# First retention output projection: first column pair by seven block products, interleaved with the next head's q and k, and the shared residual memory in two halves

## Chip, cores and metric

The kernel runs on one core of a Trainium2 chip. The metric is the device time of one execution in microseconds (us). The kernel before takes 1374.24 us (median of 3 runs, 1373.81 to 1374.61).

## What is computed

A decoder trunk of two layers over 256 tokens and a width of 2048: first gated linear attention (GLA), then retention. Both project the normalised input to q, k, v and a gate, mix over the tokens by head, multiply by the SiLU of the gate and project back with an output matrix; a residual add follows. The retention layer has 8 heads with 256 key and 512 value columns each.

```python
h = x
h = h + gla_mixer(rms_norm(h, gla_norm), ...)
h = h + retention_mixer(rms_norm(h, ret_norm), positions, ...)
return rms_norm(h, final_norm)

def retention_mixer(h, positions, w_in, gn_g, gn_b, w_out):
    q, k, v, gate = jnp.split(h @ w_in, ...)      # 8 heads
    q, k = apply_rotary(q, cos, sin), apply_rotary(k, cos, sin)
    ...                                           # decayed scores @ v, group norm
    return (o * jax.nn.silu(gate)) @ w_out        # (256 x 4096) @ (4096 x 2048)
```

## The kernel before

**Work of one weight block.** The weights come in blocks ("subs") of 256 contraction rows by 512 columns, 512 KB each. SP loads a block into a `raw` buffer (L260). ACT copies it, rounded, to `hi` (L298), DVE writes the rest, raw minus hi, to `lo` (L299), and PE multiplies three times: activations-hi by hi, hi by lo, and lo by hi (`mm3`, `three`: L340 to L342 and L411 to L413). There are four `hi` and four `lo` buffers, and `next_weights` keeps three blocks ahead (LOOK). The list of all loads and blocks is fixed by `_plan`, which also gives each load its buffer: eight `raw` buffers, and two more (`lc` and `qk`, the SPARE table) in stages where the tiles that own them are idle.

**Direct and seven-product pairs.** A 512-column output for all 256 tokens takes 12 matmuls of 512 columns a block (two token halves, two 128-row tiles, three terms) and eight blocks, so two column groups take 192. A *pair* (`pair` in `_plan`, `out_pair`, `values_and_gates`) treats two column groups at once. The second half of the contraction is done directly (tokens v4 to v7 for one group, g4 to g7 for the other, 12 matmuls each). The first half is a 2x2 block product that is done with seven block products instead of eight (P1, P2, P3, P5, P6, P7, P8, each of two blocks and 12 matmuls). So a pair takes 96 + 84 = 180 matmuls, but 22 blocks: products read a block for 6 matmuls only. Four products use sums of activation blocks (`make_sums`, four tiles), and their weight sums are made by adding one raw block to another: by DVE (L293, before P6) and by accumulating DMAs that POOL issues (L310), six a pair. Results of products that enter two outputs are added to the residual straight from PSUM (`join`, L990 and L992), 512 columns each.

**The stages around the change.** Retention head h consists of eight q/k blocks (`step_w`: eight matmuls of 512 columns and eight of 256 a block) and one pair for v and gate. In heads 1 to 3 and 5 to 7 the two are interleaved (order MIXED), in heads 0 and 4 all q/k blocks come first (WHOLE). The attention work of a head (`ret_tasks`: rotary, scores, norm, transposes into `ogt`) is spread over the next stage. The output projection is done in two halves of the contraction: after heads 0 to 3 ("ra", this is where the change lies) and after heads 4 to 7 ("rb"). In ra, column groups 0 and 1 are direct (`out_half` with CUT: six blocks of group 0, six of group 1, then the rest, since head 3 is still being finished), and groups 2 and 3 are a pair (`out_pair(2)`). The sums of `ogt` (`rsum`) are made in the direct part.

**One memory, two tenants.** The `rs` memory (16 KB a partition, one buffer) holds in turn the residual (256 tokens by 2048) and the four sums of the layer's input `xhl` (`sums`), both 2 MB. Before ra the sums are in it, with a copy in HBM (`keep_sums`, L469). `get_resid` (L480, POOL) brings the residual, after ra `put_resid` (L485, ACT's queue) writes it to HBM, and `reload_sums` (L476, POOL) brings the sums back for head 4, whose first use of them is P3, after eight q/k blocks.

**Order.** Each engine works through its instructions in the order in which they stand. A scheduler at build time moves some of them; `keep` pins what must not move. DMAs that POOL issues stand in POOL's order, so one that must wait holds up those behind it.

Of the kernel before, what the change touches and what calls it, by code (L numbers as in the profile page):

```python
# [57 lines left out]
SPARE = {"lc": ("ao", "rqk", "rv", "rg", "ro"), "qk": ("ao", "ro")}  # L58


def _spare(load):
    return [NRAW + n for n, kinds in enumerate(SPARE.values()) if load[0][0] in kinds]


def _plan():
# [96 lines left out]
def ret_order(h):  # L162
    return MIXED if h % 4 else WHOLE
# [15 lines left out]
def kernel(  # L179
# [252 lines left out]
    def sums_in_rs(name):  # L432
        s = rs_p.tile([P, 4, QK, 2, P], F32R, tag="rs", name=name)
        cur["s_whole"] = s
        return lambda n: s[:, 2 * n : 2 * n + 2]
# [30 lines left out]

    def keep_sums(name):
        kept = dram_p.tile([P, 4 * QK * 2 * P], F32R, tag=name, name=f"{name}_kept")
        keep(nc.gpsimd.dma_start(kept, cur["s_whole"].rearrange("p i k a t -> p (i k a t)")))  # L469
        cur["kept"] = kept  # L470

    def reload_sums(name):
        room = sums_in_rs(name)
        cur["s"] = [room(i // 2)[:, i % 2] for i in range(4)]
        s = cur["s_whole"]
        nc.gpsimd.dma_start(s.rearrange("p i k a t -> p (i k a t)"), cur["kept"])  # L476

    def get_resid(name):
        r = rs_p.tile([P, 2, D], F32, tag="rs", name=name)
        nc.gpsimd.dma_start(r, cur["resid_at"])  # L480
        cur["resid"] = r

    def put_resid(name):
        at = dram_p.tile([P, 2, D], F32, tag=name, name=name)
        nc.scalar.dma_start(at, cur["resid"])  # L485
        cur["resid_at"] = at
# [19 lines left out]
    cur["resid"] = rs_p.tile([P, 2, D], F32, tag="rs", name="resid")  # L506
# [90 lines left out]
    def square_sum(t, c):  # L597
        junk = sg_p.tile([P, GW], F32, tag="sg", name="sqj")
        return nc.scalar.activation(
            junk, cur["resid"][:, t, c * GW : (c + 1) * GW], AF.Square, accum_out=ssum[:, t, c : c + 1]  # L600
# [43 lines left out]
    def gate_low_rank():  # L644
        for t in range(2):
            keep(nc.sync.dma_start(cur["resid"][:, t, :], x_n[:, t, :]))
# [311 lines left out]
    def out_cols(c, ps, t, first, final):  # L958
        dst = cur["resid"][:, t, c * GW : (c + 1) * GW]
# [8 lines left out]
    def out_transposes(c):  # L968
        return transpose_out(
            lambda t, j: cur["resid"][:, t, c * GW + j * P : c * GW + (j + 1) * P],  # L970
# [6 lines left out]
    def out_pair(c, first, name, final=False):  # L977
# [9 lines left out]
        def join(col, t, src, op=ALU.add):  # L987
            dst = cur["resid"][:, t, col * GW : (col + 1) * GW]
# [7 lines left out]
        def whole(col, t, now=False):  # L996
# [5 lines left out]
            if final:  # L1002
                keep(a)
                dst = cur["resid"][:, t, col * GW : (col + 1) * GW]
# [13 lines left out]
        direct(lhs, (C, V1), 4)  # L1018
        join(g, 0, A)
# [48 lines left out]
    def out_last(name):  # L1068
# [10 lines left out]
        for t in range(2):  # L1079
            dst = cur["resid"][:, t, 3 * GW : 4 * GW]  # L1080
# [41 lines left out]
    def out_tail():  # L1122
# [4 lines left out]
        for t in range(2):  # L1127
# [20 lines left out]
            for n in range(2):  # L1148
                dst = cur["resid"][:, t, base + n * half : base + (n + 1) * half]
# [9 lines left out]
            for piece, src, which in (  # L1159
# [6 lines left out]
                src = cur["resid"][:, t, piece] if src is None else src  # L1166
# [137 lines left out]
    def ret_head(h):  # L1304
        lhs = xhl
        mixed = h % 4 != 0
        at = (2, 3, 0, 1) if h < 4 else (0, 1, 2, 3)
        q_ps = [acc(1, f"rqk{h}_ps{c}", (P, 2, SEQ), [at[c + 2]])[0] for c in range(2)]
        q_ps += [lev_p.tile([P, 2, SEQ], F32, tag="lev", name=f"rqk{h}_ps{c}") for c in (2, 3)]
        if not mixed:  # L1310
            q_ps = q_ps[2:] + q_ps[:2]
        r, r2 = r2_[:, 0, :], r2_[:, 1, :]
# [17 lines left out]

        def tile_of(key, pool_, shape, dtype, name):
# [14 lines left out]
        def turn(tok):  # L1346
            n = toks.index(tok)
            if n == drain:
# [113 lines left out]
    slots = deque((0, 1, 2, 3))  # L1462
# [115 lines left out]
```

## Time and profile before

| What | Value |
|---|---|
| median of the runs | 1374.24 us |
| the profiled execution | 1373.05 us, of which its span (first to last instruction) is 1371.3 us |
| PE busy | 1362.1 us (99%), 6564 matmuls |
| DVE / ACT / POOL busy | 1099.5 (80%) / 845.8 (62%) / 136.8 us (10%) |
| granted TensorE clock | 0.998 |
| moved by DMA | 315.03 MB, mean 230 GB/s |
| head 3 / ra direct / ra pair / q,k of head 4 / pair of head 4 | first matmul at 855.7 / 918.9 / 967.7 / 1008.7 / 1031.0 us |

The profile names groups of instructions by line, engine, operation and tile (buffer numbers left out); "<-" in a bracket names who ended the idle time before. PE's matmuls overlap, so the duration of one is more than its share of the time; how far apart they start is its share. An instruction that issues a DMA is short, and the time to landing is listed apart.

### The profile page before, as it was taken

To read this page: it belongs to the slowest core of one execution; us is meant where nothing else is said; L and a number is where in the kernel's file an instruction comes from. 1 tells how busy PE (TensorE), PEld (TensorE's weight loads), DVE (VectorE), ACT (ScalarE), POOL (GpSimd) and SP (SyncE) were. 2 spreads that over 40 slices of the span, in tenths; PEclk is the share of its full clock that TensorE was granted. 3 is DMA by queue.
4 is the path that set the end of the run, shared out by engine and by line. 5 is a ranking of instruction groups with operands and counts; after the bars stand their busy time and mean duration, and the time that the engine had idled before them with its cause. 6 is when DMAs were issued, how large, how long until landed. Compare 5 with 4: busy or idle time off the path is not lost.

```text
span 1371.3 us, 18373 instructions
## 1 busy us (share of the span) xinstructions
PE 1362.1 (99%) x6564; PEld 1144.2 (83%) x6564; DVE 1099.5 (80%) x1523; ACT 845.8 (62%) x1115; POOL 136.8 (10%) x194
## 2 busy tenths in 40 slices
PE   9999999999999999999999999999999999999997
PEld 8888888888888888888888888888888888888886
DVE  7686795987878896869888888897867897889796
ACT  6576656656567757656666566655546666666565
POOL 1003020110021021001011010100101101010010
PEclk9999999999999999999999999999999999999999
DMA  9755565789658667868897878796798797869773
GB/s 367 254 173 167 171 206 184 162 245 320 196 153 265 203 205 176 322 169 236 271 324 198 259 201 252 207 321 210 176 360 225 239 262 198 254 201 323 234 179 121
DMA packets 84507, 315.03 MB, mean 230 GB/s; under 512 B 9776, under 2 KB 10800, under 8 KB 83136
## 3 DMA queue, kind: packets, MB, share of 16 engines
q1 hardware_dynamic: 67200, 241.63, 50.3%
q0 software_dynamic: 15920, 64.89, 23.8%
q10 hardware_dynamic: 1296, 7.35, 1.5%
q8 instruction: 51, 0.84, 0.2%
q14 instruction: 40, 0.33, 0.1%
HBM read 303.35 MB, written 10.49 MB: 229 GB/s over the span
## 4 chain that ended last, share of the span: by engine, by line
PE 99%; DVE 0%; ACT 0%; issue 0%; DVEq 0%; POOL 0%; POOLq 0%
PE rqk_ps L383 8%; PE re_ps L411 8%; PE re_ps L412 8%; PE re_ps L413 8%; PE rqk_ps L384 4%; PE gqk_ps L383 4%; PE gg_ps L341 3%; PE gv_ps L342 3%; PE gv_ps L340 3%; PE gv_ps L341 3%; PE gg_ps L340 3%; PE gg_ps L342 3%; PE ge_ps L413 2%; PE ge_ps L411 2%; PE ge_ps L412 2%; PE gae_ps L413 2%
## 5 line engine op out<-in xcount | busy, mean ns | idle before, releaser
L299 DVE TENSOR_TENSOR lo<-raw,hi 128x1024 fp32r<-128x1024 f32 (+1 forms) x567 | 686.6, 1221 | 215.8 <-ACT hi L298 206.7
L298 ACT ACTIVATE hi<-raw 128x1024 fp32r<-128x1024 f32 (+1 forms) x567 | 595.7, 1057 | 396.5 <-DMA raw<-in_w_all 53.4
L383 PE MATMUL rqk_ps<-xhl,hi 128*128 128x512 f32 x480 | 162.8, 397 | 0.0
L412 PE MATMUL re_ps<-lo,xhl 128*128 128x512 f32 x352 | 137.3, 390 | 0.0
L413 PE MATMUL re_ps<-hi,xhl 128*128 128x512 f32 x352 | 137.1, 389 | 0.0
L310 POOL DMA_DIRECT2D raw<-in_w_all x90 | 78.0, 868 | 555.4 <-DVE lo L299 354.3
L411 PE MATMUL re_ps<-hi,xhl 128*128 128x512 f32 x352 | 132.4, 391 | 0.0
L384 PE MATMUL rqk_ps<-xhl,lo 128*128 128x256 f32 x480 | 122.3, 280 | 0.0
L383 PEld LDWEIGHTS rqk_ps<-xhl,hi 128*128 128x128 f32 x480 | 89.5, 188 | 17.9
L384 PEld LDWEIGHTS rqk_ps<-xhl,lo 128*128 128x128 f32 x480 | 87.5, 189 | 3.4
L413 PEld LDWEIGHTS re_ps<-hi,xhl 128*128 128x128 f32 x352 | 66.1, 188 | 13.7
L412 PEld LDWEIGHTS re_ps<-lo,xhl 128*128 128x128 f32 x352 | 66.1, 188 | 13.1
L411 PEld LDWEIGHTS re_ps<-hi,xhl 128*128 128x128 f32 x352 | 66.0, 188 | 13.2
L383 PE MATMUL gqk_ps<-xhl,hi 128*128 128x512 f32 x216 | 76.6, 399 | 0.0
L341 PE MATMUL gg_ps<-lo,xhl 128*128 128x512 f32 x192 | 75.4, 393 | 0.0
L341 PE MATMUL gv_ps<-lo,xhl 128*128 128x512 f32 x192 | 75.2, 392 | 0.0
L340 PE MATMUL gv_ps<-hi,xhl 128*128 128x512 f32 x192 | 75.1, 393 | 0.0
L342 PE MATMUL gv_ps<-hi,xhl 128*128 128x512 f32 x192 | 75.0, 391 | 0.0
L342 PE MATMUL gg_ps<-hi,xhl 128*128 128x512 f32 x192 | 74.9, 390 | 0.0
L340 PE MATMUL gg_ps<-hi,xhl 128*128 128x512 f32 x192 | 74.8, 391 | 0.0
L828 POOL TENSOR_TENSOR s<-s,m 128x64 f32<-128x64 f32 x56 | 36.1, 677 | 232.6 <-DVE m L819 223.3
L384 PE MATMUL gqk_ps<-xhl,lo 128*128 128x256 f32 x216 | 59.0, 280 | 0.0
(434 smaller groups left out, 2656.4 us busy)
## 6 DMA issues: line engine op xcount, KB each, us to landing
raw<-in_w_all SPq DMA_DIRECT2D x449, 512.0 KB, 4.8
raw<-in_w_all POOLq DMA_DIRECT2D x90, 512.0 KB, 6.8
resid<-in_x_n SPq DMA_DIRECT2D x2, 1024.0 KB, 10.0
gg<-in_gn_g POOLq DMA_DIRECT2D x8, 256.0 KB, 4.1
resid_x<-resid ACTq DMA_DIRECT2D x1, 2048.0 KB, 7.8
gb<-in_gn_b POOLq DMA_DIRECT2D x8, 256.0 KB, 6.1
gb_resid<-resid_x POOLq DMA_DIRECT2D x1, 2048.0 KB, 11.0
resid_g<-gb_resid ACTq DMA_DIRECT2D x1, 2048.0 KB, 9.3
```

The costliest lines, as they stand in the source:

```text
L298: a = nc.scalar.activation(hi[:, sl], src[:, sl], AF.Copy)
L299: b = nc.vector.tensor_tensor(lo[:, sl], src[:, sl], hi[:, sl].bitcast(F32), ALU.subtract)
L310: nc.gpsimd.dma_start(raws[n], block(key), accum_op=ALU.add)
L340: pin(mm(ps, xh, hi[:, q, :], start=kt == begin, stop=False))
L341: pin(mm(ps, xh, lo[:, q, :], start=False, stop=False))
L342: pin(mm(ps, xl, hi[:, q, :], start=False, stop=kt == end - 1))
L383: mm(ps[c], wh, rhs[:, kt, :, :], start=kt == 0, stop=False)
L384: mm(ps[c][:, 0, :], wl, rhs[:, kt, 0, :], start=False, stop=False)
L411: pin(mm(ps, xh, hi[:, q, :], start=start, stop=False, **again))
L412: pin(mm(ps, xh, lo[:, q, :], start=False, stop=False, **again))
L413: pin(mm(ps, xl, hi[:, q, :], start=False, stop=stop, **again))
L828: nc.gpsimd.tensor_tensor(dst, dst, side_of(m[:, li, :], z), ALU.add)
```

## The change

1. Column groups 0 and 1 of ra become a seven-product pair, in an order of its own (NEXT) in which the eight q/k blocks of head 4 are interleaved. Head 4 keeps only its v and gate pair (order UNIT), behind `out_pair(2)`.
2. The `rs` memory becomes two buffers of 8 KB a partition, rs0 and rs1: column groups 0 and 1 of the residual, or sums 0 and 1, and groups 2 and 3, or sums 2 and 3. All loads and stores of either are split in two 1 MB DMAs.
3. The exchange at the end of ra is done by halves (`swap`), each a store and a reload on POOL's queue: half 0 inside `out_pair(2)` after its first direct block, half 1 inside head 4 after its block v4. The store of the residual moves from ACT's queue to POOL's.
4. In ra the `qk` buffer is no spare load buffer any more, since head 4's q and k are written to it.

```diff
-SPARE = {"lc": ("ao", "rqk", "rv", "rg", "ro"), "qk": ("ao", "ro")}
+SPARE = {"lc": ("ao", "rqk", "rv", "rg", "ro"), "qk": ("ao", "ro1")}
...
         if half == 0:
-            out_cols_of("ro", half, CUT, JOINT["ro", half])
+            pair(("ro", 0, 1), ("ro", 0, 0), ("rqk", 4), NEXT)
+            pair(("ro", 0, 3), ("ro", 0, 2))
...
 def ret_order(h):
-    return MIXED if h % 4 else WHOLE
+    return MIXED if h % 4 else (UNIT if h else WHOLE)
+
+NEXT = "q0 q1 q2 q3 P1 q4 z q5 P5 q6 q7 P6 P2 P3 v4 v5 v6 P7 v7 g4 g5 P8 g6 g7"
...
+    def put_resid(name, ns=range(2), eng=nc.scalar):
+        if 0 in ns:
+            cur["resid_at"] = []
+        for n in ns:
+            at = dram_p.tile([P, 2, HD], F32, tag=f"{name}{n}", name=f"{name}{n}")
+            eng.dma_start(at, cur["resid"][n])
+            cur["resid_at"].append(at)
...
+    def out_pair_with_next(c, name, q_step, at):
+        A, B = (acc(1, f"{name}e{c}_ps{n}", which=[at[n]])[0] for n in range(2))
...
+        for tok in NEXT.split():
+            kind, last = tok[0], tok[1:] == str(NSUB - 1)
...
+            if kind == "q":
+                q_step(int(tok[1:]))
+                step(2 if int(tok[1:]) < 3 else 1)
+            elif tok == "P1":
+                product(A, plain(0, 0), stop=True)
+                join(g, 0, A)
+            elif tok == "P2":
+                product(B, plain(4, 0))
+            elif tok == "P3":
+                product(C(2), summed(0))
+            elif tok == "P5":
+                product(B, summed(1), stop=True)
+                for t in range(2):
+                    join(c, t, B)
...
+            elif tok == "P6":
+                while tasks:
+                    step()
+                product(A, summed(2), stop=True)
+                join(c, 0, A, ALU.subtract)
+            elif tok == "P7":
+                product(A, summed(3), stop=True)
...
+            elif tok == "P8":
+                product(A, plain(4, 1))
+            else:
+                direct(lhs, (C(2), C(3)) if kind == "v" else (B, A), int(tok[1:]), stop=last)
...
         def turn(tok):
             n = toks.index(tok)
+            if h == 4 and tok == "v4":
+                swap(1)
...
-    out_half(True, False, "ra", CUT, out_steps, JOINT["ro", 0])
-    put_resid("resid_r")
+    get_resid("ra_resid")
+    q_step, box = q_and_k(4, (0, 1))
+    out_pair_with_next(0, "ra", q_step, (2, 3, 0, 1))
+    slots = deque((3, 0, 1, 2))
+
+    def swap(n):
+        put_resid("resid_r", [n], nc.gpsimd)
+        reload_sums("sums2", [n])
+
+    out_pair(2, True, "ra", after=lambda: swap(0))
     if True:
-        reload_sums("sums2")
         for h in range(4, 8):
-            ret_head(h)
+            ret_head(h, box if h == 4 else None)
```

What this does to the order on the engines is shown at two places. The number behind `hi`, `lo` and `rae` names the block or the column group, the number at the end a buffer. L299 of before is L304 of the changed kernel.

**Place 1, the middle of ra.** DVE before, while PE works on the last blocks of groups 0 and 1: a `lo` for every 12 matmuls, with the sums between them.

```order
L299 TENSOR_TENSOR lo385_8410<-raw313_8233,hi385_8409 128x1024
L463 TENSOR_TENSOR rsum0_8425<-rsum_f0_8383,rsum0_8425 128x4x128 x2
L299 TENSOR_TENSOR lo386_8433<-raw314_8253,hi386_8432 128x1024
L463 TENSOR_TENSOR rsum1_8448<-rsum_f1_8384,rsum1_8448 128x4x128 x2
L299 TENSOR_TENSOR lo387_8456<-raw315_8273,hi387_8455 128x1024
L299 TENSOR_TENSOR lo388_8474<-raw316_8298,hi388_8473 128x1024
```

DVE now, between P5 and P3 (blocks 386 and 387 are P6, 388 and 389 are P2; `rae0_ps1` is the PSUM bank B of P5 and then of P2).

```order
L304 TENSOR_TENSOR lo386_8455<-raw306_8070,hi386_8454 128x1024
L304 TENSOR_TENSOR lo387_8468<-raw307_8124,hi387_8467 128x1024
L1024 TENSOR_TENSOR ra_resid0_8242<-rae0_ps10_8251,ra_resid0_8242 128x512 x2
L472 TENSOR_TENSOR rsum1_8488<-rsum_f1_8365,rsum1_8488 128x4x128 x2
L304 TENSOR_TENSOR lo388_8494<-raw314_8315,hi388_8493 128x1024
L1416 TENSOR_TENSOR rqk4_8515<-rqk4_ps2_8248,rqk4_h2_8516 128x256
L1416 TENSOR_TENSOR rqk4_8515<-rqk4_ps3_8249,rqk4_h2_8516 128x256
L1416 TENSOR_TENSOR rqk4_8515<-rqk4_ps00_8246,rqk4_h2_8516 128x256
L1416 TENSOR_TENSOR rqk4_8515<-rqk4_ps10_8247,rqk4_h2_8516 128x256
L304 TENSOR_TENSOR lo389_8526<-raw315_8346,hi389_8525 128x1024
```

PE at the same place: the end of q7, the first matmuls of P6, and one of P2 that stands among them.

```order
L385 MATMUL rqk4_ps10_8247<-xhl_106,lo385_8443 128x256
L386 MATMUL rqk4_ps10_8247<-xhl_106,hi385_8442 128x512
L416 MATMUL rae0_ps00_8250<-hi386_8454,rsum1_8488 128x512
L417 MATMUL rae0_ps00_8250<-lo386_8455,rsum1_8488 128x512
L416 MATMUL rae0_ps10_8251<-hi388_8493,ogt_107 128x512
L418 MATMUL rae0_ps00_8250<-hi386_8454,rsum1_8488 128x512
```

The two adds of P5's result to the residual, the last two sums and the four adds that finish head 4's q and k now stand between the `lo` of products, and the third matmul of this stretch waits for P5's bank to be read.

**Place 2, POOL at the end of ra.** Before, the reload of the sums is one DMA, followed by the six accumulating loads of head 4.

```order
L310 DMA raw318_8341<-in_w_all 128x1024
L310 DMA raw319_8365<-in_w_all 128x1024
L476 DMA sums2_8887<-sums_kept_6357 128x4096
L310 DMA raw340_8847<-in_w_all 128x1024
L310 DMA raw341_8865<-in_w_all 128x1024
```

Now the second store and the second reload stand between the first two and the other four accumulating loads of head 4.

```order
L315 DMA raw338_8944<-in_w_all 128x1024
L315 DMA raw339_8956<-in_w_all 128x1024
L515 DMA resid_r1_9162<-ra_resid1_8243 128x2048
L490 DMA sums21_9164<-sums_kept1_6370 128x2048
L315 DMA raw341_8981<-in_w_all 128x1024
L315 DMA raw342_8999<-in_w_all 128x1024
```

The store waits for the last add to the residual of `out_pair(2)`, the reload for the store's landing, and head 4's P6, 73 matmuls behind the last one of `out_pair(2)`, for the reload.

More of the change, by code (lines that the diff above doesn't have):

```diff
@@ L645, in gate_low_rank @@
         for t in range(2):
-            keep(nc.sync.dma_start(cur["resid"][:, t, :], x_n[:, t, :]))
+            for n in range(2):
+                keep(nc.sync.dma_start(cur["resid"][n][:, t, :], x_n[:, t, n * HD : (n + 1) * HD]))
             yield
@@ L978, in out_pair @@
+    def out_pair(c, first, name, final=False, after=None):
         lhs, s = ogt, cur["s"]
@@ L1018, in out_pair @@
         direct(lhs, (C, V1), 4)
+        if after is not None:
+            after()
         join(g, 0, A)
@@ L1165, in out_tail @@
             ):
-                src = cur["resid"][:, t, piece] if src is None else src
+                src = resid_part(t, piece.start, piece.stop) if src is None else src
                 if which == "v":
```

117 lines of the change are left out of this document (82 added, 35 removed).

## The prediction

> **What bounds the kernel now.** I read the page's busy times and its chain of waits first.
>
> ```profile
> span 1371.3 us, 18373 instructions
> PE 1362.1 (99%) x6564; PEld 1144.2 (83%) x6564; DVE 1099.5 (80%) x1523; ACT 845.8 (62%) x1115; POOL 136.8 (10%) x194
> PE 99%; DVE 0%; ACT 0%; issue 0%; DVEq 0%; POOL 0%; POOLq 0%
> ```
>
> The chain that ended last is PE from end to end, and PE is busy for all but 9.2 us. So the time is the number of matmuls times their spacing, plus the waits that an edit adds or takes away; there is hardly a wait left to take away. What a matmul is worth is its spacing, which the timeline of PE shows in the direct part of ra. These are the first two and the last of 72 matmuls in a row.
>
> ```profile
> 926.40 0.39 PE L342 MATMUL ra_ps<-hi,ogt 128*128 128x512 f32 x1
> 926.62 0.39 PE L340 MATMUL ra_ps<-hi,ogt 128*128 128x512 f32 x1
> ...
> 942.49 0.39 PE L341 MATMUL ra_ps<-lo,ogt 128*128 128x512 f32 x1
> ```
>
> (942.49 - 926.40) / 71 = 0.2266 us, though each lasts 0.39 us, since they overlap. In q and k blocks wide and narrow ones alternate:
>
> ```profile
> 1009.15 0.40 PE L383 MATMUL rqk_ps<-xhl,hi 128*128 128x512 f32 x1
> 1009.39 0.28 PE L384 MATMUL rqk_ps<-xhl,lo 128*128 128x256 f32 x1
> 1009.51 0.40 PE L383 MATMUL rqk_ps<-xhl,hi 128*128 128x512 f32 x1
> ```
>
> There a wide one takes 0.24 us and a narrow one 0.12.
>
> **What the change removes.** Groups 0 and 1 of ra take 180 matmuls instead of 192, and the eight q/k blocks of head 4 are only moved. 12 x 0.2266 = 2.72 us less on PE, -0.20%. This is the most that the change can bring by what it removes, unless a wait of before goes with it, and ra has none: PE's spacing there is even.
>
> **What it adds beside PE.** The pair has 22 weight blocks where the direct part had 16, so six more `hi` on ACT and `lo` on DVE, two adds of raw blocks on DVE, and nine joins instead of four. How full DVE is shows in the table by stretch; its columns are length, PE, PEld, DVE, ACT, POOL, clock, DMA share and GB/s.
>
> ```profile
> 864.00:900.00 36.00, 36.00 (x186) 30.63 (x185) 29.31 (x32) 21.80 (x26) 3.46 (x4) 1.00 0.81 233
> 918.70:967.60 48.90, 48.90 (x221) 40.56 (x220) 34.76 (x51) 24.97 (x33) 2.86 (x4) 1.00 0.71 212
> 967.60:1008.90 41.30, 41.30 (x184) 34.21 (x184) 34.68 (x35) 23.88 (x24) 3.45 (x4) 1.00 0.84 249
> ```
>
> The first row is the stretch of head 3 in which q and k blocks alternate with P5, P6, P2 and P3, the nearest thing to the new order; DVE idles there for 6.7 of 36 us. The new order has the same blocks and, besides, four sums and three more joins in such a stretch (P1's, which falls into it, and P5's two; P6's has a counterpart in head 3), 7 x 0.6 = 4.2 us (durations below). On the average it fits, with 2.5 us to spare. But three products, P6, P2 and P3, now follow each other, where the old orders put q blocks between P6 and P2, and the order on DVE (place 1) puts joins and sums between their `lo`. So I add up this place by hand, from these rows:
>
> ```profile
> 879.21 1.06 ACT L298 ACTIVATE hi<-raw 128x1024 fp32r<-128x1024 f32 x1 [1.35 <-PE rqk_ps L383]
> 880.30 2.52 DVE L299 TENSOR_TENSOR lo<-raw,hi 128x1024 fp32r<-128x1024 f32 x2 [1.19 <-ACT hi L298]
> 886.79 1.54 DVE L1323 TENSOR_TENSOR rqk<-rqk_ps,rqk_h 128x256 f32<-128x256 f32 x4
> 917.38 3.49 DVE L299 TENSOR_TENSOR lo<-raw,hi 128x1024 fp32r<-128x1024 f32 x3
> 920.78 0.55 DVE L723 TENSOR_TENSOR rsc<-rs,rsc 128x384 fp32r<-128x384 f32 x1
> 948.34 1.29 DVE L463 TENSOR_TENSOR rsum<-rsum_f,rsum 128x512 fp32r<-128x512 f32 x2
> 961.94 1.28 DVE L960 TENSOR_TENSOR ra_resid<-ra_ps,ra_resid 128x512 f32<-128x512 f32 x2
> ```
>
> A `lo` follows the `lo` before it after (920.78 - 917.38) / 3 = 1.13 us and ends after 1.22; a sum or a join takes 0.60 and ends after 0.68; the four adds of q and k take 1.46. A `hi` takes 1.06, its `lo` starts at its end, and it waits until PE has let go of the buffer of four blocks before.
>
> Time zero is the start of the last matmul on P5's first block. That buffer is free at 0.39, `hi386` is ready at 1.45. From there DVE, in its order: `lo386` 1.13, a wait for `hi387` 0.25 (its buffer comes free six matmuls later: 6 x 0.2266 + 0.39 + 1.06 = 2.81), `lo387` 1.13, two joins 1.2, two sums 1.2, `lo388` 1.13, q and k 1.46, `lo389` and `lo390` 2.26, a join 0.6, and `lo391` ready after 1.22: 13.0 us. PE, without a wait, is at the first matmul that needs `lo391` (the second of P3's second block) after 7 on P5 (1.59), q7's last 4 wide and 8 narrow (0.96 + 0.96), and 32 wide ones (7.25): 10.8 us. **PE loses 13.0 - 10.8 = 2.2 us**, about 1.4 of it at the first matmul of P2 that stands within P6 and waits for the joins of P5. Behind P3 come direct blocks, 12 matmuls or 2.72 us for one `lo` each, and DVE catches up. The bounds of this term: nothing, if the average decides (head 3's order loses nothing), and 4.2 us, if all the added DVE work ends on the path. I take 2.2.
>
> **The exchange by halves.** The store of half 0 and its reload have 207 matmuls (47 us) up to head 4's P3: hidden. Half 1 has less. What the two take is seen best in the old exchange.
>
> ```profile
> 1008.46 0.39 PE L413 MATMUL rae_ps<-hi,ogt 128*128 128x512 f32 x1
> 1008.18 1.40 DVE L990 TENSOR_TENSOR ra_resid<-rae_ps,ra_resid 128x512 f32<-128x512 f32 x2
> 1009.61 0.33 ACTq L485 DMA_DIRECT2D resid_r<-ra_resid  x1
> 1019.77 0.55 POOL L476 DMA_DIRECT2D sums<-sums_kept  x1 [35.96 <-DVE lo L299]
> resid_r<-ra_resid ACTq DMA_DIRECT2D x1, 2048.0 KB, 9.4
> sums<-sums_kept POOLq DMA_DIRECT2D x1, 2048.0 KB, 12.0
> sums_kept<-sums POOLq DMA_DIRECT2D x1, 2048.0 KB, 7.8
> ra_resid<-resid_g POOLq DMA_DIRECT2D x1, 2048.0 KB, 9.1
> raw<-in_w_all POOLq DMA_DIRECT2D x90, 512.0 KB, 6.8
> raw<-in_w_all SPq DMA_DIRECT2D x449, 512.0 KB, 4.8
> resid<-in_x_n SPq DMA_DIRECT2D x2, 1024.0 KB, 10.0
> ```
>
> The last matmul of the pair starts at 1008.46 and the store is issued 1.15 us later; the reload is issued 0.76 us after the store has landed (1009.61 + 9.4 = 1019.0). Head 4's P6 stands 73 matmuls behind, 16.5 us, so store and reload together have 14.6 us. Two DMAs of 2 MB took 9.4 + 12.0 = 21.4, 6.8 too long; two of 512 KB on SP's queue take 9.6, two accumulating ones 13.6. The only row of 1 MB says 10.0 each, 5.4 too long together, but both stood among the loads of the start. Between 4.8 for 512 KB and the mean of 9.6 of the four rows of 2 MB, 1 MB lies at 4.8 + (9.6 - 4.8) / 3 = 6.4, two at 12.8: in time by 1.8 us. I take nothing for this term and keep 0 to 6.8. Behind the waiting store and reload on POOL stand the accumulating loads for head 4's P7 and P8. They need the `lo` of P6, four blocks ahead of PE at most, so they come after the reload's issue anyway.
>
> The Trainium skill (DMA: Bandwidth & Descriptors, "Anatomy of one DMA") prices a DMA of POOL at about 2.0 us plus its bytes at 436 GB/s. As an estimate from that page, 1 MB takes 4.4 us, two 8.8, and the reload would never be late. The trace does not follow it: 2 MB by it is 6.8 us and took 7.8 to 12.0 beside the weight loads.
>
> **Costed at nothing.** The loads of head 4's q and k and of the new pair use nine raw buffers; head 3's did too, with the same blocks per matmul, at a DMA share of 0.81 and 233 GB/s and no loss on PE. The pair's second half now has nine instead of ten; head 4's pair had nine. The halved DMAs add an issue each (0.33 us on ACT's queue, 0.55 on POOL), on engines that idle 38% and 90% of the time. If the supply fell short, ACT's `hi` would wait for DMA and each block lost would cost PE 1.4 to 2.7 us.
>
> **The sum** against the profiled execution's own 1373.05 us (span 1371.3 and 1.75 around it): 1373.05 - 2.72 + 2.2 = 1372.5. The median of the runs lies 1.2 above that execution, so 1373.7 to be compared with 1374.24.
>
> **Rivals.** *Full gain*: DVE is ahead enough, or the wait at P2 is absorbed; 1374.24 - 2.72 = 1371.5. For it speaks that the same work fits in head 3; against it that the chain above starts at a buffer PE itself frees, so no lead of DVE helps. *Late reload*, the one on the slow side: store and reload of half 1 take longer than 14.6 us and PE stands before head 4's P6. It decides at 7.3 us a DMA. At the 7.8 of the fastest 2 MB row it costs 1 us, at 10.0 5.4 and at the old exchange's pair 6.8; with the DVE wait that is 1374.7 to 1380.5. For it speak the slow rows just quoted, and that DMA moves 212 to 249 GB/s there already; against it the size halved. It would eat the gain from 0.5 us on.
>
> The Trainium skill (TensorE: Matmul & The Clock Gate, "Part 1: The HAM clock gate") adds that PE's clock halves when PE has idled through a window of 3.4 us. By that a long wait here would cost up to 1.7 us more, an estimate; no run here shows it, since PE's 9.2 us of idling are spread over the span.
>
> **How the numbers follow.** About 0.2% (2.7 us) is what a measurement of this kernel can tell from no change. Forecast 0.42 (own range 1372.3 to 1375.5, all within 0.2%). Full gain 0.18; since 2.72 us is just that bound, half of it counts as faster. Late reload 0.34, of which 0.22 beyond +2.7 us. Another loss of the same kind elsewhere (accumulating loads landing late for P7, a supply gap) 0.06, counted as slower. Faster 0.09, same 0.42 + 0.09 + 0.12 = 0.63, slower 0.28. The range 1371.3 to 1378.3 leaves out the worst reloads.
>
> **What would show it.** In the profile after: 6552 matmuls; spacing of 0.2266 except between P5 and P3 of ra's first pair, where PE waits for DVE's joins, sums and `lo`, 2.2 us in all; head 4's P6 starting 16.5 us after the last matmul of the pair, or later if the reload is late; store and reload at 6.4 us each. I am wrong if PE shows no gap between P5 and P3, if the gap exceeds 4.2 us, or if PE waits elsewhere.

## The result and the profile after

The changed kernel takes 1379.74 us (median of 11 runs, 1374.49 to 1384.11) where the kernel before takes 1374.24. The ratio is 1.0040, 95% interval 1.0030 to 1.0049: slower by 5.5 us, and 1.4 us above the upper end of the forecast's range (1371.3 to 1378.3). Its runs scatter over 9.6 us, those of before over 3.2. The profiled execution took 1379.93 us.

The head of its page, against 1371.3 us and 6564 matmuls before, and the chain that ended last:

```profile
span 1378.2 us, 18418 instructions
PE 1364.3 (99%) x6552; PEld 1141.2 (83%) x6552; DVE 1109.8 (81%) x1536; ACT 850.9 (62%) x1122; POOL 142.1 (10%) x207
PE 79%; issue 13%; DMA 3%; DVE 2%; POOL 1%; ACT 1%; SPq 0%; POOLq 0%; DVEq 0%; ACTq 0%
```

There are 12 matmuls fewer, as forecast, and still the chain is no longer PE alone. To find where PE stands still I add up, for all consecutive matmuls, the distance between their starts less the median distance of that width (0.2266 us at 512 columns). I call this PE's loss. Over the whole span it is 9.4 us before and 19.0 after, 9.7 more; less the 2.72 us of the 12 matmuls that makes 7.0, and the spans differ by 6.9. So the loss holds the whole difference, and the stage where it arises can be read off: 3.5 us in the new pair, 3.6 more in `out_pair(2)`, 1.2 in head 4, 0.9 in ga (the first layer's first output projection, far ahead of the change), 0.5 in small pieces.

**The new pair, between P5 and P3.** PE's timeline at the place that the prediction worked out by hand; the third row is the matmul of P2 that stands within P6:

```profile
953.27 0.40 PE L416 MATMUL rae_ps<-hi,rsum 128*128 128x512 f32 x1
953.50 0.39 PE L417 MATMUL rae_ps<-lo,rsum 128*128 128x512 f32 x1
954.29 0.47 PE L416 MATMUL rae_ps<-hi,ogt 128*128 128x512 f32 x1 [0.40 <-DVE ra_resid L1024]
954.80 0.50 PE L418 MATMUL rae_ps<-hi,rsum 128*128 128x512 f32 x1
```

It starts 0.79 us after the one before it instead of 0.23, and waits for the join of P5. Between 945 and 965 us PE loses 1.6 us. The table by stretch shows why, first of the kernel before, then of the changed one (length, PE, PEld, DVE, ACT, POOL, clock, DMA share, GB/s):

```profile
943.00:965.00 22.00, 22.00 (x102) 18.27 (x102) 14.61 (x16) 11.12 (x14) 0.90 (x1) 1.00 0.58 175
```

```profile
943.00:965.00 22.00, 21.52 (x106) 17.13 (x105) 22.00 (x27) 14.98 (x21) 3.45 (x4) 1.00 0.67 166
```

DVE, which was busy for 14.6 of these 22 us, has no idle moment left. A second loss follows 10 us later, at P7. Here are POOL's two accumulating loads for P7, what each took to land (first of the load at 960.37, then of the one at 962.28), ACT's `hi` of these blocks, and PE:

```profile
960.37 0.86 POOL L315 DMA_DIRECT2D raw<-in_w_all  x1 [6.26 <-DVE lo L304]
962.28 0.85 POOL L315 DMA_DIRECT2D raw<-in_w_all  x1 [1.04 <-DVE lo L304]
```

```profile
raw<-in_w_all POOLq DMA_DIRECT2D x1, 512.0 KB, 7.2
```

```profile
raw<-in_w_all POOLq DMA_DIRECT2D x1, 512.0 KB, 9.4
```

```profile
967.64 1.06 ACT L303 ACTIVATE hi<-raw 128x1024 fp32r<-128x1024 f32 x1 [4.75 <-DMA raw<-in_w_all]
971.77 3.90 ACT L303 ACTIVATE hi<-raw 128x1024 fp32r<-128x1024 f32 x4 [3.07 <-DMA raw<-in_w_all]
```

```profile
972.89 0.50 PE L416 MATMUL rae_ps<-hi,rsum 128*128 128x512 f32 x1 [0.23 <-ACT hi L303]
974.15 0.50 PE L417 MATMUL rae_ps<-lo,rsum 128*128 128x512 f32 x1 [0.76 <-DVE lo L304]
```

The loads may be issued only when P3's `lo` has been made, the second landed at 962.28 + 9.4 = 971.7, and the `hi`, the `lo` and the matmul follow one after the other. That costs another 1.5 us.

**`out_pair(2)`.** POOL, then the mean landing of the two loads for its P7 before and after, then ACT and PE:

```profile
993.15 0.56 POOL L515 DMA_DIRECT2D resid_r<-ra_resid  x1 [3.19 <-DVE ra_resid L1024]
1003.36 0.55 POOL L490 DMA_DIRECT2D sums<-sums_kept  x1 [9.64 <-DMA resid_r<-ra_resid]
1004.03 1.80 POOL L315 DMA_DIRECT2D raw<-in_w_all  x2
```

```profile
raw<-in_w_all POOLq DMA_DIRECT2D x2, 512.0 KB, 6.7
```

```profile
raw<-in_w_all POOLq DMA_DIRECT2D x2, 512.0 KB, 9.9
```

```profile
1012.62 1.06 ACT L303 ACTIVATE hi<-raw 128x1024 fp32r<-128x1024 f32 x1 [1.95 <-DMA raw<-in_w_all]
1016.38 2.95 ACT L303 ACTIVATE hi<-raw 128x1024 fp32r<-128x1024 f32 x3 [2.70 <-PE rae_ps L418]
```

```profile
1018.44 0.79 PE L416 MATMUL rae_ps<-hi,ogt 128*128 128x512 f32 x1 [2.06 <-ACT hi L303]
```

The reload of half 0 went out 0.7 us ahead of the loads, and they took 3.2 us longer than before. The second ACT row names PE; the matmuls on that buffer were over by 1012.8, so what came last was the second load, which landed 11.4 us after its issue, at 1016.3. The matmul that waits reads `ogt`: it is the first of the direct block g4, which the build put ahead of P7, as it did before. Its `hi` stands on ACT behind that of P7's second block. PE waited 2.06 us, and then this, from the table by stretch:

```profile
1018.00:1019.00 1.00, 0.56 (x1) 0.29 (x1) 1.00 (x2) 1.00 (x2) 0.00 (x0) 0.69 1.02 270
1019.00:1020.00 1.00, 0.88 (x3) 0.56 (x3) 1.00 (x2) 0.33 (x1) 0.00 (x0) 0.50 1.06 295
1020.00:1021.00 1.00, 1.00 (x4) 0.81 (x3) 1.00 (x2) 0.00 (x0) 0.00 (x0) 0.50 1.08 279
1021.00:1022.00 1.00, 1.00 (x4) 0.77 (x4) 0.56 (x1) 0.00 (x0) 0.00 (x0) 0.60 1.07 258
1022.00:1023.00 1.00, 1.00 (x6) 0.83 (x5) 0.00 (x0) 0.85 (x1) 0.00 (x0) 1.00 1.03 283
```

The granted clock (third number from the right) falls to 0.50 from 1018.4 to 1021.8 us: four matmuls per microsecond. About 1.6 of the 4.1 us lost here are the clock's.

**Half 1.** Store and reload on POOL, then the last matmul of `out_pair(2)` and head 4's P6 on PE:

```profile
1038.00 0.56 POOL L515 DMA_DIRECT2D resid_r<-ra_resid  x1 [3.06 <-DVE ra_resid L1084]
1045.48 0.54 POOL L490 DMA_DIRECT2D sums<-sums_kept  x1 [6.92 <-DMA resid_r<-ra_resid]
```

```profile
1036.48 0.39 PE L418 MATMUL rae_ps<-hi,ogt 128*128 128x512 f32 x1
1053.38 0.47 PE L416 MATMUL re_ps<-hi,sums 128*128 128x512 f32 x1 [0.19 <-DMA sums<-sums_kept]
```

Store and reload took 7.2 and 7.8 us. P6 comes 16.9 us after the last matmul, 0.35 later than without a wait.

**ga.** ACT's queue, before and after: the store of the residual there is now two, and the first has moved 42 us ahead, into a pair.

```profile
334.35 0.34 ACTq L485 DMA_DIRECT2D resid_x<-resid  x1
```

```profile
292.93 0.33 ACTq L515 DMA_DIRECT2D resid_x<-resid  x1
335.28 0.33 ACTq L515 DMA_DIRECT2D resid_x<-resid  x1
```

### The profile page after: what moved, and what is told of

Its sections match the earlier page's. It is cut to its first block, busy times and chain, and to the rows that moved or that the text cites. A ratio compares the mean times of both kernels' runs of the same rounds, so it can differ in the third digit from the quotient of the medians.

```text
span 1378.2 us, 18418 instructions
## 1 busy us (share of the span) xinstructions
PE 1364.3 (99%) x6552; PEld 1141.2 (83%) x6552; DVE 1109.8 (81%) x1536; ACT 850.9 (62%) x1122; POOL 142.1 (10%) x207
## 4 chain that ended last, share of the span: by engine, by line
PE 79%; issue 13%; DMA 3%; DVE 2%; POOL 1%; ACT 1%; SPq 0%; POOLq 0%; DVEq 0%; ACTq 0%
PE rqk_ps L388 5%; PE re_ps L417 4%; PE re_ps L416 4%; PE re_ps L418 4%; PE gqk_ps L388 4%; DMA raw<-in_w_all 3%; PE gg_ps L347 3%; PE gv_ps L345 3%; PE gv_ps L346 3%; PE gv_ps L347 3%; PE gg_ps L345 3%; PE gg_ps L346 3%; PE rqk_ps L389 3%; PE ge_ps L417 2%; PE ge_ps L418 2%
## 5 line engine op out<-in xcount | busy, mean ns | idle before, releaser
L304 DVE TENSOR_TENSOR lo<-raw,hi 128x1024 fp32r<-128x1024 f32 (+1 forms) x573 | 693.0, 1221 | 210.0 <-ACT hi L303 201.7
L315 POOL DMA_DIRECT2D raw<-in_w_all x96 | 83.5, 872 | 583.1 <-DVE lo L304 361.2
L417 PEld LDWEIGHTS re_ps<-lo,xhl 128*128 128x128 f32 x352 | 66.1, 188 | 14.3 <-DVE lo L304 1.2
L418 PEld LDWEIGHTS re_ps<-hi,xhl 128*128 128x128 f32 x352 | 66.1, 188 | 13.6
L859 POOL TENSOR_TENSOR s<-s,m 128x64 f32<-128x64 f32 x56 | 32.4, 610 | 235.2 <-DVE m L850 221.9
## 6 DMA issues: line engine op xcount, KB each, us to landing
gb_resid<-resid_x POOLq DMA_DIRECT2D x2, 1024.0 KB, 10.3
```

The lines of the kernel that those rows point to most:

```text
L304: b = nc.vector.tensor_tensor(lo[:, sl], src[:, sl], hi[:, sl].bitcast(F32), ALU.subtract)
L315: nc.gpsimd.dma_start(raws[n], block(key), accum_op=ALU.add)
L417: pin(mm(ps, xh, lo[:, q, :], start=False, stop=False, **again))
L418: pin(mm(ps, xl, hi[:, q, :], start=False, stop=stop, **again))
L859: nc.gpsimd.tensor_tensor(dst, dst, side_of(m[:, li, :], z), ALU.add)
```

## The experiments

Times are medians, ratios are to the kernel before on the same chip (its medians there: 1374.06 to 1374.28). The column "profiled" is the time of the one execution that was profiled, and the right part is PE's loss in it, us, by stage: start (to 40), ga (285 to 345), new pair (925 to 986), `out_pair(2)` (986 to 1036), head 4 (1036 to 1085), all. The profiled execution can lie far from the median: that of "both halves on SP" was the fastest of 12, that of "P7 behind v7" the slowest of 11.

| Kernel | us | ratio (95%) | profiled | start | ga | new pair | pair(2) | head 4 | all |
|---|---|---|---|---|---|---|---|---|---|
| before | 1374.24 | 1 | 1373.05 | 3.6 | 0.0 | 0.0 | 0.5 | 0.1 | 9.4 |
| changed | 1379.74 | 1.0040 (1.0030 to 1.0049) | 1379.93 | 3.7 | 0.9 | 3.5 | 4.1 | 1.3 | 19.0 |
| changed, again | 1378.30 | 1.0031 (1.0019 to 1.0042) | 1378.19 | 3.6 | 2.2 | 3.9 | 0.8 | 1.6 | 17.3 |
| reload behind | 1379.57 | 1.0034 (1.0022 to 1.0046) | 1380.03 | 4.2 | 2.7 | 2.2 | 1.6 | 2.7 | 19.2 |
| half 0 on SP | 1378.67 | 1.0030 (1.0018 to 1.0042) | 1377.86 | 4.2 | 2.2 | 2.7 | 0.4 | 1.1 | 16.6 |
| probe | 1380.91 | 1.0045 (1.0033 to 1.0057) | 1382.06 | 4.1 | 3.0 | 2.8 | 0.0 | 3.5 | 21.1 |
| q7 between | 1378.92 | 1.0036 (1.0022 to 1.0050) | 1381.82 | 4.4 | 3.1 | 2.8 | 5.0 | 0.4 | 21.0 |
| stores pinned | 1378.32 | 1.0027 (1.0013 to 1.0040) | 1380.68 | 4.4 | 0.6 | 1.9 | 5.1 | 0.8 | 19.8 |
| both halves on SP | 1376.98 | 1.0025 (1.0015 to 1.0035) | 1374.22 | 4.2 | 0.7 | 2.5 | 0.2 | 0.3 | 13.1 |
| pinned and SP | 1375.40 | 1.0013 (1.0004 to 1.0022) | 1374.77 | 4.0 | 0.8 | 2.3 | 0.5 | 0.8 | 13.6 |
| pinned and SP, again | 1376.46 | 1.0013 (1.0004 to 1.0022) | 1375.44 | 3.5 | 0.9 | 2.2 | 1.0 | 1.5 | 14.3 |
| halves alone | 1375.77 | 1.0008 (1.0000 to 1.0017) | 1376.06 | 3.8 | 0.9 | 0.0 | 1.7 | 0.0 | 12.1 |
| halves pinned | 1374.14 | 0.9997 (0.9988 to 1.0006) | 1374.51 | 4.2 | 0.5 | 0.0 | 0.5 | 0.1 | 10.6 |
| P5 apart | 1379.85 | 1.0035 (1.0022 to 1.0048) | 1379.85 | 3.8 | 0.8 | 2.7 | 3.7 | 2.0 | 19.0 |
| pinned, SP and P5 apart | 1376.43 | 1.0017 (1.0008 to 1.0026) | 1374.85 | 4.2 | 0.4 | 2.6 | 0.4 | 0.7 | 13.7 |
| P7 behind v7 | 1374.51 | 1.0002 (0.9992 to 1.0011) | 1377.87 | 3.8 | 0.9 | 2.1 | 4.1 | 0.0 | 16.7 |
| sums early | 1374.91 | 1.0007 (0.9997 to 1.0016) | 1375.45 | 4.3 | 0.9 | 1.5 | 1.7 | 0.8 | 14.3 |
| both edits | 1374.59 | 0.9999 (0.9990 to 1.0008) | 1372.79 | 4.0 | 0.8 | 0.2 | 0.5 | 0.9 | 11.6 |

Experiments 1 to 4, and 9, ran on one chip, 5 and the first kernel of 6 on another, 7, 8 and the second kernel of 6 on a third.

My theory after the result: the reload of half 0 in POOL's DMA queue makes P7's loads late. Its rivals: POOL's order of issue, the bandwidth whatever the queue, and the pair itself.

**1. The reload behind the loads.**

```diff
-    out_pair(2, True, "ra", after=lambda: swap(0))
+    out_pair(
+        2, True, "ra",
+        after=lambda: put_resid("resid_r", [0], nc.gpsimd),
+        later=lambda: reload_sums("sums2", [0]),
+    )
...
         product(A, summed(2), stop=True)
         product(B, plain(4, 0))
+        if later is not None:
+            later()
```

The reloads are pinned besides; on the five engines only this reload changes its place.

> One instruction moved: the reload of half 0 is issued by POOL behind the four accumulating loads of out_pair(2) instead of ahead of them; PE's, DVE's, ACT's and SP's orders are those of the changed kernel. In the changed kernel's trace PE loses 4.1 us between 1015 and 1022 us, where P7 of out_pair(2) waits for two accumulating loads that landed 8.5 and 11.4 us after their issue (before: 5.2 and 8.3). Theory Queue (the megabyte of the reload goes through POOL's DMA queue ahead of them): they land in 5 to 8.5 us, that loss falls below 1 us, the time by 3 to 4 us from 1379.7 to 1376 +- 0.7. Theory Order (POOL waits with the reload for the store's landing, and the loads are issued late): the same gain, with the loads issued 1 us earlier or more. Rival Pair (the loss belongs to the new pair's own order): no change, 1379 or more.

The two loads landed sooner (8.0 against 9.9), and the loss in `out_pair(2)` fell from 4.1 to 1.6 us. But 1.6 us remain with no reload ahead of the loads, and the time stayed, 1379.57. Two places show where the gain went. One is ga, far ahead of the edit: it lost 2.7 us in this profile, 0.9 in that of the changed kernel, so the times of experiments 1 to 4 hold a loss that their edits do not touch (2.2 to 3.1 us). The other is P6 of head 4, which waits for the reload of half 1:

```profile
raw<-in_w_all POOLq DMA_DIRECT2D x2, 512.0 KB, 8.0
```

```profile
1052.60 0.47 PE L416 MATMUL re_ps<-hi,sums 128*128 128x512 f32 x1 [0.97 <-DMA sums<-sums_kept]
```

**2. Half 0 on SP's queue.**

```diff
     def swap(n):
-        put_resid("resid_r", [n], nc.gpsimd)
-        reload_sums("sums2", [n])
+        eng = (nc.sync, nc.gpsimd)[n]
+        put_resid("resid_r", [n], eng)
+        reload_sums("sums2", [n], eng=eng)
```

> Store and reload of half 0 are issued by SP at the same places of the program, so POOL's queue holds only the accumulating loads there. Theory Queue: as with the reload behind, 3 to 4 us less than the changed kernel, 1376 +- 0.7, or even a little more since the store leaves the queue too. Rival Bandwidth (the same bytes at the same time fill the DMA engines, whatever the queue): the accumulating loads still land in 8 us and more, and the time stays within 1 us of 1379.7. A cost of its own is possible in both: SP's weight loads stand behind the store's and the reload's waits, which shows as ACT's hi waiting for SP's loads.

The loss in `out_pair(2)` is 0.4 us; the time fell by 1.1, less than a third of what was expected and within the scatter.

**3. POOL waits, but its queue is empty.** As in 1, and at the reload's old place a DMA of 2 KB that reads what was stored.

```diff
+    def store_and_wait():
+        put_resid("resid_r", [0], nc.gpsimd)
+        probe = st_p.tile([P, 4], F32, tag="sq", name="probe")
+        nc.gpsimd.dma_start(probe, cur["resid_at"][0][:, 0, 0:4])
```

> As the reload behind, but at the reload's old place POOL issues a DMA of 2 KB that reads the stored half, so POOL waits for the store's landing as in the changed kernel while almost nothing goes through its queue. (The 2 KB are read into a scratch tile that nothing uses.) Theory Queue: as the reload behind, within 0.7 us of it, near 1376.5. Theory Order: the loss comes back, the time is that of the changed kernel, 1379 or more.

POOL did wait, and issued the loads as late as in the changed kernel, 0.7 us after the wait:

```profile
1005.03 0.56 POOL L1583 DMA_DIRECT2D probe<-resid_r  x1 [9.15 <-DMA resid_r<-ra_resid]
1005.71 1.88 POOL L315 DMA_DIRECT2D raw<-in_w_all  x2
```

```profile
raw<-in_w_all POOLq DMA_DIRECT2D x2, 512.0 KB, 7.2
```

```profile
1053.28 0.47 PE L416 MATMUL re_ps<-hi,sums 128*128 128x512 f32 x1 [2.01 <-DMA sums<-sums_kept]
```

PE lost nothing in `out_pair(2)`. So POOL's order of issue alone makes no loss there, and in this profile the loads land sooner without the megabyte beside the first of them; one profile alone does not settle it (8). The time again did not fall (1380.91): head 4 lost 3.5 us, 2.2 of them before P6 (its first matmul starts 2.4 us after the one before it; the store of half 1 took 11.1 us for 7.2), ga lost 3.0, and the runs scatter from 1377.0 to 1382.9. The local part of the theory holds; its price in the whole is not seen in the time.

**4. q7 between P6 and P2.**

```diff
-NEXT = "... z q5 P5 q6 q7 P6 P2 P3 v4 ..."
+NEXT = "... z q5 P5 q6 P6 q7 P2 P3 v4 ..."
```

> In the new pair's order q7 stands between P6 and P2 instead of ahead of P6; nothing else is changed. In the changed kernel's trace PE loses 1.6 us between 950 and 970 us (DVE's chain of joins, sums, q and k adds and lo ahead of P2 and P3) and 1.5 us at P7 of the pair, whose two accumulating loads POOL could issue only after P3's lo (960.4 and 962.3 us) and which landed 7.2 and 9.4 us later. Theory DVE (P7's loss is a second bill of the same late lo): both fall, to under 1 us together, and the time by 2 to 2.7 us to 1377.4 +- 0.7. Rival Late landings (P7's loss comes from slow loads and not from DVE): the loss at P7 stays at 1 us or more, the gain is 1 us or less, 1378.7 or more.

Not as expected. P7's loss went, but 2.4 us stand ahead of P3 now instead of 1.6: the loss of the pair only moved.

**5. Stores pinned, and both halves on SP.** Three kernels: the pins, SP for both halves, and the two together.

```diff
-            eng.dma_start(at, cur["resid"][n])
+            put = eng.dma_start(at, cur["resid"][n])
+            if eng is nc.scalar:
+                keep(put)
```

> One line: the stores of the residual after ga and gb (ACT's queue) are pinned to their place in the program. In the changed kernel the first half's store had moved 25 ACT rows up in ga and 36 in gb, into the pair: it is issued at 293 and 613 us instead of at the end of the stage (335 and 657). All other engines' orders stay. In the five profiles with that store PE loses 0.9, 2.7, 2.2, 3.0 and 3.1 us between 285 and 345 us (mean 2.4), before 0.02, and 0.2 to 1.0 between 605 and 660 (mean 0.57), before 0.22. Theory Early store (1 MB moved beside the pair's accumulating loads makes them land late): the loss in ga falls below 0.3 us, the one in gb to 0.2, the time by 2.2 to 2.9 us to 1377.2 +- 0.7. Rival Scatter (ga's losses are chance and have nothing to do with the store): the loss stays, the time too, 1379 or more.

> As with half 0 on SP, and half 1's store and reload too. In the profiles so far head 4 loses 1.3, 2.7, 1.1, 3.5 and 0.4 us, part of it before P6 (the reload late), part at P7 and the blocks around it (four accumulating loads that land 9 to 17 us after their issue behind the reload). Theory Queue: PE loses below 0.5 us in out_pair(2) and below 0.7 in head 4, and the time is 0.4 to 1.2 us under that with half 0 on SP (1378.67): 1377.8 +- 0.6. Rival Bandwidth: head 4 still loses 1.1 us or more, and the time is 1378.7 or more.

> The two before together: stores after ga and gb pinned, both halves of the exchange on SP. If the losses add: 1377.8 - 2.4 = 1375.4 +- 0.8; what is left above before less 2.72 us (1371.6) is then the new pair's own loss of 2.2 to 3.5 us, 0.5 us at the start and head 4. If the early stores are chance: 1377.5 or more.

With the exchange on SP the losses in `out_pair(2)` and head 4 are 0.2 and 0.3 us in the profile (the fastest execution), and the median is 1376.98; with the pins it is 1375.40. The pins alone gave 1378.32, between what the two theories expected. (The changed kernel itself did not run on this chip.) On this chip the pins show nothing in ga: it lost 0.7 us with the early store (both halves on SP) and 0.6 and 0.8 with the pins. But the chip of the first four experiments, where ga lost 2.2 to 3.1 us with the early store, ran four kernels with pins later (9), and there ga lost 0.8 to 0.9. Over all profiles ga lost 0.4 to 0.9 us in the eight with pins; in the nine with the early store it lost 0.7 to 0.9 in four and 2.2 to 3.1 in five. So the early store can cost ga some 2 us, and often does not.

**6. Halves alone, without and with pins.** The kernel before, with only the memory in two halves; then all its stores pinned as in 5.

> The kernel before with the memory in two halves and nothing else of the change: columns 0 and 1 direct, head 4 with q and k first, PE's 6564 matmuls. The scheduler may move the first halves' stores and the first reload up (it puts them in ga, gb and the pair of ra). Theory Halves (most of the slowdown comes from 1 MB transfers beside accumulating loads, and little from the pair): 1374.3 + 2.4 (ga) + 0.4 (gb) + 0.5 (start) + 1 to 4 (pair of ra) = 1377.6 to 1381, PE losing in ga and in the pair of ra. Rival Pair (the interleaved pair makes the loss): within 0.7 us of before, 1373.6 to 1375.

> The kernel before with the memory in two halves and all stores pinned at the end of their stages, so no 1 MB transfer stands in a pair. Halves alone without the pins was 1375.77, with PE losing 1.7 us in the pair of ra, 0.9 in ga and 0.8 in gb. Theory Early store: these fall to 0.5, 0.6 and 0.2, the time to 1374.3 +- 0.5, that of before. Rival Chance: 1375.5 or more.

Halves alone are slower by 1.6 us than before on its chip, much less than expected; pinned, the kernel is as fast as the one before (0.9997). So the halves cost nothing that can be told apart but for the transfers that move ahead on their own. The intervals of the two overlap (1.0000 to 1.0017, 0.9988 to 1.0006), so the 1.6 us between them are likely, not certain.

**7. P5 apart.** P5 gets a bank of its own, and its joins stand behind P3; once in the changed kernel, once on top of 5.

```diff
-                product(B, summed(1), stop=True)
-                for t in range(2):
-                    join(c, t, B)
+                P5 = mis_p.tile([P, GW], F32, tag="mis", name=f"{name}e{c}_p5")
+                product(P5, summed(1), stop=True)
...
                 product(C(2), summed(0))
+                for t in range(2):
+                    join(c, t, P5)
```

> The changed kernel with P5 in a bank of its own and its joins behind P3, nothing else. Theory DVE chain: PE's loss in the pair, 2.2 to 3.5 us in the profiles so far, falls below 1 us, the time by 1.2 to 2.5 us against the changed kernel in the same call. Rival Supply: the loss in the pair stays above 1.7 us, the time within 0.7 us.

> Stores pinned, the exchange on SP, and in the new pair P5 gets a PSUM bank of its own, so that its two joins (1.2 us on DVE) stand behind P3's lo and the first matmul of P2 waits for no join. In the profile of the kernel without this PE loses 1.3 us between 950 and 965 us and 0.6 at P7. Theory DVE chain: the first falls by about 1.2 us to some tenths, P3's lo and with them P7's loads come 1.2 us earlier and P7's loss goes too: 1375.4 - 1.6 = 1373.8 +- 0.7, no slower than before. Rival Supply (PE waits there for loads, and DVE's order only decides where): the loss stays above 1.7 us in the pair, 1375 or more.

Neither came out as expected. On top of 5 the loss from 950 to 965 us fell from 1.3 to 0.15, as expected, but 1.1 us appeared in the q blocks just ahead (945 to 950), where P5's matmuls now stood later and PE waited for `lo`, and P7 still lost 0.9.

**8. The changed kernel again**, on the chip of 7 and of halves pinned.

> The changed kernel itself on this chip, beside the three others. Median 1378.5 to 1380.5, scatter 5 us or more; by the theory Queue PE loses 3 us or more in out_pair(2), 2 to 3.5 in the new pair, 0.7 to 3 in ga, and these losses differ from profile to profile. If the median is below 1377 here, the differences between the kernels of the earlier calls can't be told from differences between chips.

Here `out_pair(2)` lost only 0.8 us, not the 3 or more expected, with the same program. What differs is the store of half 0, which landed 7.8 us after its issue instead of 9.9, so that the reload left 1.5 us ahead of P7's loads instead of 0.7, and the second of these loads, which landed 10.3 after its issue instead of 11.4.

**9. The pair's own loss.** On top of 5: P7 one block later (the join of its copy moves along); the second halves of the sums no longer pinned, so that the build puts them some 40 rows earlier on DVE; both; and the base again on the same chip.

```diff
-NEXT = "... P6 P2 P3 v4 v5 v6 P7 v7 g4 g5 P8 g6 g7"
+NEXT = "... P6 P2 P3 v4 v5 v6 v7 P7 g4 g5 P8 g6 g7"
...
-            keep(nc.scalar.activation(s[i][:, :, 0, :], x, AF.Copy))
-            keep(tt(s[i][:, :, 1, :], x, s[i][:, :, 0, :].bitcast(F32), ALU.subtract))
+            pin = (lambda n: n) if name == "rsum" else keep
+            pin(nc.scalar.activation(s[i][:, :, 0, :], x, AF.Copy))
+            pin(tt(s[i][:, :, 1, :], x, s[i][:, :, 0, :].bitcast(F32), ALU.subtract))
```

> Stores pinned and the exchange on SP, and in the new pair P7 stands behind v7, one direct block (12 matmuls, 2.7 us) later; nothing else. Without it PE loses 0.6 to 1.9 us at P7 in the profiles, where the two accumulating loads, issued after P3's lo at 960 to 962 us, land 7 to 9.6 us later, as PE comes to P7. Theory Late P7 loads: 2.7 us more of time take this loss to 0.1 or less, the 1.3 us ahead of it (DVE) stay; the time falls by 0.6 to 1.0 us against the same kernel without it in this call. Rival DVE full: DVE is busy for 21.9 of the 22 us from 943 to 965, so the loss only moves to another block of the pair, no change.

> Stores pinned and the exchange on SP, and the second halves of the four sums of ogt are not pinned: the scheduler puts these four DVE subtractions (2.4 us) and four ACT copies some 40 rows up, ahead of the new pair, where DVE idles 4.6 of 10 us (920 to 930). Theory DVE full: DVE's work between 943 and 965 falls from 21.9 to about 19.5 us, PE's loss of 1.3 us ahead of P3 to some tenths, and since P3's lo and P7's loads come 1 to 2 us earlier, P7's too; pair below 0.6 us in all, time 1.5 to 2 us less than without. Rival Supply: the loss stays above 1.5 us.

> The two edits before together (P7 behind v7, sums early). If each takes its part: PE loses 0.3 us or less in the pair, the time is 1373.3 +- 0.6, faster than before by 0.5 to 1.5 us; left over against 1374.24 - 2.72 are 0.5 at the start, 0.5 in ga and 0.7 in head 4 and out_pair(2). If DVE or the supply only moves the loss: 1374.5 or more.

> Stores pinned and the exchange on SP, as before (1375.40), on this chip: the base for the three others. 1375.4 +- 0.7, pair 2.2 to 2.7 us of loss.

The stretch from 943 to 965 us, with the sums early, then with both edits:

```profile
943.00:965.00 22.00, 22.00 (x112) 18.62 (x111) 20.16 (x24) 12.91 (x16) 4.02 (x5) 1.00 0.79 195
```

```profile
943.00:965.00 22.00, 22.00 (x111) 18.61 (x111) 20.99 (x25) 13.98 (x17) 3.87 (x5) 1.00 0.83 197
```

With the sums early DVE has 1.8 us to spare, PE is busy for all of it, and the loss from 945 to 965 us, 1.4 and 1.9 in the two profiles of the base, is gone (0.1); PE comes to P7 earlier and loses 1.2 there. With P7 one block later alone, P7 loses nothing and 1.8 ahead stay. With both the pair loses 0.2 us: it has two losses, and each edit takes one. The medians do not show that the two add up: 1374.51 and 1374.91 alone, 1374.59 (0.9999) together, 1.9 us under the base and as long as before, where 1373.3 +- 0.6 was expected. No version beat the kernel before by what can be told apart.

The profile with P7 behind v7 shows one thing more. The exchange is on SP there, and yet `out_pair(2)` lost 4.1 us:

```profile
raw<-in_w_all POOLq DMA_DIRECT2D x2, 512.0 KB, 10.0
```

```profile
1016.55 0.50 PE L416 MATMUL rae_ps<-hi,ogt 128*128 128x512 f32 x1 [1.58 <-ACT hi L303]
```

The store took 10.2 us in that execution (8.3 to 9.3 in the others with half 0 on SP), and the reload left 0.13 us ahead of the loads instead of 1.0 to 1.5:

```profile
1001.75 0.33 SPq L490 DMA_DIRECT2D sums<-sums_kept  x1
1001.88 0.88 POOL L315 DMA_DIRECT2D raw<-in_w_all  x1 [13.32 <-DVE raw L298]
```

Over all profiles with the reload ahead of the loads, on either queue, the same order shows: where it left 0.1 to 0.8 us ahead (five profiles), `out_pair(2)` lost 3.7 to 5.0 us; where it left 1.0 to 1.5 us ahead (eight), 0.2 to 1.7; with the reload behind the loads it was 1.6 and 0.0. By this it is not the queue that counts but how much of the reload's megabyte runs beside P7's loads, and with SP the short lead was rarer (one of eight, against four of five on POOL). No run sets this lead alone, and what lengthens the store is not known.

## Why the prediction was wrong

1. *What the change removes* was right: 6552 matmuls, 2.72 us.
2. *The wait between P5 and P3* was right in place and mechanism, 1.6 us instead of 2.2. Of the 1.4 expected at P2's first matmul 0.6 stand there. That DVE's full stretch makes this loss is shown by the sums early: the average over 36 us, which left 2.5 us to spare, said nothing of 22 us without a pause.
3. *"Behind P3 come direct blocks, and DVE catches up"* holds for DVE, but it was taken to end the matter. P7's loads wait for P3's `lo`. POOL issued the second of them 10.2 us before PE could have used its block (in head 3 of before 11.6), and it took 9.4 to land (there 7.2), with `hi` and `lo` still to be made: 0.8 us were left for these where head 3 had 4.4. This second bill is 1.5 us; it comes and goes (0.0 in one profile of the base, 1.2 with the sums early), and with P7 behind v7 it was 0.0 both times. The prediction held it, within "another loss elsewhere", at 0.06.
4. **The step that failed is "the store of half 0 and its reload have 207 matmuls (47 us): hidden."** The reload itself was hidden. What shares the DMA with it was not asked: P7's loads of `out_pair(2)`, with about 2 us to spare at their 6.7 us. They took 9.9, PE lost 3.6 us more than before, some 1.6 of them by the clock; in the second profile of the same kernel it was 0.4 more. This is the largest single loss of the profile that stands beside the result, and not of every execution. For half 1 the loads behind were named, but only their issue was looked at.
5. *Half 1's exchange* was mis-sized: store and reload took 7.2 and 7.8 us for 6.4 each, 15.0 where there was room for 14.6, and the wait at P6 is 0.35 instead of 0; it was 1.1 and 2.2 in two experiments, well inside the rival's bounds. Most of the rest of head 4's 1.2 lies at P7 and just ahead, where the four loads behind the reload landed after 9.2 to 17.1 us (7.1 to 13.8 before); that they are its cause was not tried alone.
6. *"Costed at nothing: the halved DMAs add an issue each"* failed too. A smaller tile is final earlier, so its store is free to move, and the build put the first halves' stores of ga and gb 42 and 45 us ahead, into pairs. Halves alone against halves pinned puts some 1.6 us on all such moves, with intervals that overlap.

The two sides of the forecast that held most of the chance, DVE and a late reload, were real and small. What decided is one thing that neither held: accumulating loads that land late, in several pairs, partly because of transfers that are not late themselves. That is shown for `out_pair(2)`, likely for ga, and only argued for head 4.

## What to carry to other kernels

A transfer that is early enough for its own reader still has a price if it runs beside loads with little slack: list the loads under way while it runs, and how long each may take. A reload that waits for a store inherits the store's scatter (7.8 to 10.9 us for half 0), and the loads beside it inherit it from the reload; the runs of this kernel scatter by 9.6 us, those of before by 3.2. When a buffer is split, look where the scheduler puts the pieces' stores, not only at their cost of issue.

## What was not expected of the hardware

**The clock.** In five profiles PE waited 1.23 to 2.61 us ahead of P7 of `out_pair(2)` (and 0.41 again just after, in four of them), and each time the granted clock went to 0.50 for 3.41 us, from the end of that wait or up to 1.64 us later. In two others the waits were 0.66 and 0.81, and 0.41, and it stayed at 1.00. It also stayed at 1.00 after the 2.01 us ahead of P6 in experiment 3. So a wait here can cost up to 1.7 us more than its length, and the length alone does not decide. The Trainium skill (TensorE: Matmul & The Clock Gate, "Part 1: The HAM clock gate") gives a free-running window of 3413 ns, and half the clock after an idle one. The length agrees with 3.41 us; waits of 1.23 and 0.41 us, less than half a window together, were enough, so the trigger as the page words it does not agree. Where the wait falls in such a window may be what decides; no run here tests that.

**Accumulating loads.** In the profile of before, a stretch in which hardly anything but accumulating loads runs, and one with plain loads only; the DMA share is the second number from the right:

```profile
965.00:969.00 4.00, 4.00 (x19) 3.32 (x18) 2.47 (x4) 2.12 (x2) 0.88 (x1) 1.00 1.03 201
996.00:1000.00 4.00, 4.00 (x19) 3.34 (x18) 3.37 (x5) 1.70 (x2) 0.00 (x0) 1.00 1.03 420
```

At the same full share the engines move 201 GB/s against 420: in these stretches an accumulating load holds them twice as long for its bytes. This fits with how little a pair with six of them has to spare for a megabyte.

What stays open is why ga lost 2.2 to 3.1 us in five profiles (four of one chip, one of another) and 0.7 to 0.9 in four others, with the same store in the same place.
